# Five token streams in four groups at different phases, with a bf16 copy of the weights in DRAM

## The chip, the cores and the metric

The kernel runs on all 8 cores of one Trainium2 chip, the same program on each. Every core takes one prompt sequence (16 meta tokens and 2048 prompt tokens) and 16 of the 128 single-token samples, and computes the whole layer for them with all the weights. The time is that of the slowest core in device microseconds. Names: PE is TensorE's matmuls, PEld its weight loads, DVE is VectorE, ACT is ScalarE, POOL is GpSimd, SP is SyncE. A "slab" is one unit of weights, 128 partitions by up to 4096 columns, in a ring of slots in on-chip memory; POOL issues its transfer.

Some executions fall in a slower state: the four cores of a die, sometimes only two, show a lower mean clock (0.826 to 0.831 beside 0.974 to 0.976 on the other die in a run of 1937 us). "Fast" runs are those without it.

## The reference, cut to what matters

```python
def _layer(x, buf_a, buf_b, h0, p):
    x = x + 0.5 * _rmsnorm(_swiglu(_rmsnorm(x, p['g_ffn1_pre']), ...), p['g_ffn1_post'])      # FFN 1
    m, nba, nbb, hl = _mixer(_rmsnorm(x, p['g_mix_pre']), buf_a, buf_b, h0, p)                  # mixer
    x = x + _rmsnorm(m, p['g_mix_post'])
    x = x + 0.5 * _rmsnorm(_swiglu(_rmsnorm(x, p['g_ffn2_pre']), ...), p['g_ffn2_post'])      # FFN 2
    return x, nba, nbb, hl
# _mixer: u = h @ w_in, split into A_b | A_c | A_x | B_x | B_gate | gate_A | gate_B
#   y_a = (A_b * conv3(A_c * A_x)) @ w_out_a
#   y_b = (gelu(B_gate) * RG_LRU(conv4(B_x))) @ w_out_b          # a recurrence along the tokens
#   m   = (sigmoid(gate_A) * y_a + sigmoid(gate_B) * y_b) @ w_o
```

The model is 1024 wide and the FFNs 2816. The first half of the mixer is work for DVE and ACT (convolutions, gates, recurrence), the FFNs are almost all matmul. The recurrence forces the tokens of a sequence through that half in order.

## The kernel before

Three tiles of 688 to 704 tokens, each two streams of up to 352 columns. A tile goes through all its phases before the next one begins, and both streams are in the same phase. The program is a list of operations with their reads and writes, which a list scheduler in the program puts in an order for each engine at build time.

```python
TILES = [(0, 688, 0), (688, 688, 0), (1376, 688, 16)]
NSLOT = 5                                             # weight slots
...
def issue_unit(g, paced=True, dep=None):              # every slab: f32 in DRAM, cast to bf16 by the transfer
    dst = wring[:, slot, 0:n]
    src = wall[:, off:off + n]
    S.dma("pool", f"w{slot}", lambda e, dst=dst, src=src: e.dma_start(out=dst, in_=src),
          reads=(), writes=[("w", slot)], ..., extra_deps=extra)
...
def transpose_in(b, nr, dst_fn, dst_res_fn):          # inputs come token-major; PE turns them
    ...
    for kc in range(KC):
        ins = e.transpose(out, sview[0:nr, kc * 128:(kc + 1) * 128], ident[0:nr, 0:nr])
...
def evac_with_stats(bY, bS, sm, oc, dst32, dst_res, gain_col, first, last):
    act(sq, P[:, bY, 0:sm.n], AF.Square, ...)
    act(dst32[s][:, oc, 0:sm.n], P[:, bY, 0:sm.n], AF.Identity, ..., scale=gain_col)
    def stats():                                      # one ones-matmul for each of 8 blocks
        mm_group(bS, sm.n, [ones[:, :]], [sq], ..., start=first, stop=last)
...
for ti, (row0, nseq, nsamp) in enumerate(TILES):
    for sm in sms:
        norm_apply(sm, 0, rbuf_alt(sm))
    ffn(sms, 1, 2)
    mixer(ti, sms, nseq, T, 4)
    ...
    do_load(ti + 1)                                   # next tile's x, into the other of two buffers
    ffn(sms, 2, None)
    out_events += store_tile(row0, T, ns, extra_slots=last)
```

## Time and profile before

| | before |
|---|---|
| times of three runs, us | 1828.9, 1843.65, 1851.39 |
| span of the profiled slowest core, us | 1818.6 |
| PE busy / idle in it, us | 1663.4 / 155.2 |
| bf16 matmuls; f32 transposes | 10560; 304 |
| ACT table loads | 25 |
| slabs | 174, all f32 cast to bf16 |

The profile cuts the span into 40 equal slices. The two lines below are PE's busy tenths and the granted clock in tenths of full speed (9 is 90% or more):

```profile
PE   5999788898999899978889899989997978999997
...
PEclk7999899999999999989999999989998999999999
```

Each of the three tiles leaves the same mark: a few slices of 7 and 8 where both streams stand in the mixer's first half or change phase. That is what the change goes for. The DMA queues (packets, MB, share of the 16 engines' span) were half idle; q0 carries the slabs:

```profile
q0 software_dynamic: 25200, 167.26, 50.8%
q1 hardware_dynamic: 5244, 17.99, 2.9%
```

### The profile page before, as it was taken

How to read it: one execution, taken by the hardware profiler on the slowest of the kernel's cores; microseconds unless marked ns; L12 is line 12 of the kernel's file. 1: busy time of each engine (PE TensorE's matmuls, PEld its weight loads, DVE VectorE, ACT ScalarE, POOL GpSimd, SP SyncE). 2: the span in 40 equal slices, each digit the busy share in tenths (PEclk: the TensorE clock that was granted, in tenths of full speed). 3: DMA queues.
4: the chain of work that ended last, by engine and by line, in shares of the span. 5: the costliest groups of instructions: out<-in, count | busy, mean ns of one | idle time of the engine just before them, and what ended most of it. 6: DMA issues, size and time to landing. Idle time of an engine off the chain costs nothing.

```text
span 1818.6 us, 31211 instructions; the slowest of 8 cores (1806.5 to 1818.6 us)
## 1 busy us (share of the span) xinstructions
PE 1663.4 (91%) x10864; PEld 1083.4 (60%) x10864; DVE 761.8 (42%) x1660; ACT 788.1 (43%) x1631; POOL 93.0 (5%) x179
## 2 busy tenths in 40 slices
PE   5999788898999899978889899989997978999997
PEld 3666455565666666645556566666664545656665
DVE  3220789435220522078943522052207995343203
ACT  3212478657312312247865731231124777562122
POOL 0000000000000000000000000000000000000000
PEclk7999899999999999989999999989998999999999
DMA  7755633654655685543366365566555333745552
GB/s 157 128 102 105 116 71 70 115 112 93 117 102 96 135 160 95 105 92 70 70 117 114 90 116 102 96 135 135 93 100 99 68 73 69 141 80 107 98 96 78
DMA packets 30596, 187.23 MB, mean 103 GB/s; under 512 B 3430, under 2 KB 3686, under 8 KB 14316
## 3 DMA queue, kind: packets, MB, share of 16 engines
q0 software_dynamic: 25200, 167.26, 50.8%
q1 hardware_dynamic: 5244, 17.99, 2.9%
q8 instruction: 90, 1.47, 0.3%
q14 instruction: 62, 0.51, 0.1%
HBM read 343.54 MB, written 8.94 MB: 194 GB/s over the span
## 4 chain that ended last, share of the span: by engine, by line
PE 75%; DVE 9%; issue 8%; ACT 5%; DMA 2%; DVEq 0%; ACTq 0%; SPq 0%; POOLq 0%
PE P L455 73%; ACT B L475 3%; DVE hy L499 2%; DVE B L504 2%; DVE cbb L499 1%; DMA stg<-xin 1%; DMA wring<-wall 1%; PE P L584 1%; PE P L566 1%; ACT rstd L475 1%; DVE sgb L488 1%; DVE B L488 1%; DVE A L499 1%; ACT sqb L475 1%; DVE xsA L488 0%
## 5 line engine op out<-in xcount | busy, mean ns | idle before, releaser
L455 PE MATMUL P<-hy,wring 128*128 128x352 bf16 (+1 forms) x7296 | 1142.9, 317 | 79.7 <-DVE hy L499 24.5
L455 PEld LDWEIGHTS P<-hy,wring 128*128 128x128 bf16 x7296 | 721.6, 100 | 473.5 <-issue 99.6
L455 PE MATMUL P<-big,wring 128*128 128x352 bf16 (+1 forms) x2880 | 443.1, 310 | 0.0
L455 PEld LDWEIGHTS P<-big,wring 128*128 128x128 bf16 x2880 | 281.8, 98 | 141.4
L475 ACT ACTIVATE sgb<-P 128x352 f32<-128x352 f32 (+1 forms) x312 | 140.9, 458 | 479.0 <-PE P L455 465.5
L488 DVE TENSOR_TENSOR big<-P,sgb 128x352 bf16<-128x352 f32 (+1 forms) x264 | 136.7, 519 | 465.1 <-PE P L455 463.4
L475 ACT ACTIVATE B<-B 128x352 f32<-128x352 f32 (+3 forms) x318 | 183.4, 599 | 26.8 <-DVE B L499 10.1
L434 POOL DMA_DIRECT2D wring<-wall x174 | 92.3, 530 | 1678.6 <-PE P L455 1633.1
L475 ACT ACTIVATE sqb<-P 128x352 bf16<-128x352 f32 (+1 forms) x144 | 66.1, 459 | 242.9 <-PE P L455 242.8
L488 DVE TENSOR_TENSOR sgb<-hy,rstd 128x352 f32<-128x352 f32 (+1 forms) x96 | 45.4, 514 | 295.0 <-ACT rstd L475 295.0
L455 PE MATMUL P<-sqb,ones 128*128 128x352 bf16 (+1 forms) x288 | 86.9, 326 | 23.5 <-ACT sqb L475 21.5
L488 DVE TENSOR_TENSOR B<-P,B 128x352 f32<-128x352 f32 (+1 forms) x96 | 49.6, 519 | 136.5 <-PE P L455 123.0
L499 DVE SCALAR_TENSOR_TENSOR cbb<-bxb,par_sb,cbb 128x352 f32<-128x352 f32 (+2 forms) x152 | 82.6, 555 | 3.7 <-DVE SO L511 0.4
L475 ACT ACTIVATE B<-P 128x352 f32<-128x352 f32 (+2 forms) x106 | 47.8, 457 | 80.0 <-DVE hy L488 41.9
L455 PEld LDWEIGHTS P<-sqb,ones 128*128 128x128 bf16 x288 | 28.3, 99 | 53.0 <-issue 42.2
L499 DVE SCALAR_TENSOR_TENSOR A<-acx,par_sb,A 128x352 f32<-128x352 f32 (+2 forms) x104 | 56.9, 547 | 2.8
L475 ACT ACTIVATE sqb<-xsA 128x352 bf16<-128x352 f32 (+1 forms) x96 | 43.9, 488 | 29.9 <-PE P L455 15.0
L475 ACT ACTIVATE B<-P,dpar 128x352 f32<-128x352 f32 (+1 forms) x96 | 49.1, 546 | 10.9 <-PE P L455 9.7
L475 ACT ACTIVATE hy<-P,dpar 128x352 f32<-128x352 f32 (+1 forms) x96 | 52.2, 543 | 0.0
L488 DVE TENSOR_TENSOR xsA<-xsA,sgb 128x352 f32<-128x352 f32 (+1 forms) x96 | 45.6, 514 | 0.0
L475 ACT ACTIVATE B<-B,dpar 128x688 f32<-128x688 f32 (+1 forms) x48 | 41.7, 869 | 1.5
L504 DVE TENSOR_TENSOR_SCAN B<-B,CAR 128x688 f32<-128x688 f32 x24 | 39.6, 1648 | 0.8
(74 smaller groups left out, 700.9 us busy)
## 6 DMA issues: line engine op xcount, KB each, us to landing
wring<-wall POOLq DMA_DIRECT2D x126, 1024.0 KB, 8.7
wring<-wall POOLq DMA_DIRECT2D x48, 704.0 KB, 6.2
stg<-xin SPq DMA_DIRECT2D x13, 512.0 KB, 5.7
yout<-stg SPq DMA_DIRECT2D x12, 512.0 KB, 4.1
yout<-B SPq DMA_DIRECT2D x3, 512.0 KB, 2.7
B<-xin SPq DMA_DIRECT2D x2, 512.0 KB, 9.0
wrgs<-wrg POOLq DMA_DIRECT2D x1, 512.0 KB, 13.3
stout<-stg SPq DMA_DIRECT2D x1, 408.0 KB
```

The lines of the kernel that those rows point to most:

```text
L434: S.dma("pool", f"w{slot}", lambda e, dst=dst, src=src: e.dma_start(out=dst, in_=src), reads=(), writes=[("w", slot)], dur=2.0 + n * 128 * ...
L455: ins = e.matmul(out, lhs_list[k], rhs_list[k], start=(start and k == 0), stop=(stop and k == nk - 1))
L475: return S.op("act", lambda e: e.activation(out=out, in_=in_, func=func, **kw), reads=reads, writes=writes, dur=0.12 + 0.093 * nptr + fsz( ...
L488: return S.op(eng, lambda e: e.tensor_tensor(out=out, in0=in0, in1=in1, op=op), reads=reads, writes=writes, dur=vcost(eng, out, 2))
L499: return S.op(eng, lambda e: e.scalar_tensor_tensor(out=out, in0=in0, scalar=scalar, in1=in1, op0=op0, op1=op1), reads=reads, writes=write ...
L504: return S.op(eng, lambda e: e.tensor_tensor_scan(out=out, data0=d0, data1=d1, initial=init, op0=ALU.mult, op1=ALU.add), reads=reads, writ ...
L566: ins = e.transpose(out, sview[0:nr, kc * 128:(kc + 1) * 128], ident[0:nr, 0:nr])
L584: ins = e.transpose(out, srcs[kc], ident[:, :])
```

## The change

The intent is to let phases that need different engines lie side by side. The 2080 tokens become five streams of 414 to 418 columns in four groups (streams 0 and 1 are the first group), and the groups are a phase or two apart, so that one group's mixer runs beside another's FFN. Each group now reads all weights for itself, which would be 232 casts. So the first group casts and writes a bf16 copy back to DRAM, and the others read that copy, at half the bytes. Further: x comes and goes already transposed (the host reorders it), so the transposes go; the squares of the post-norms are added on DVE and summed by one ones-matmul instead of eight; scratch tiles come from pools that the scheduler assigns; three x buffers serve the five streams.

```diff
-TILES = [(0, 688, 0), (688, 688, 0), (1376, 688, 16)]
+SIZES = [418, 418, 416, 414, 414]
+GROUPS = [[0, 1], [2], [3], [4]]
+BUFSET = [0, 1, 2, 0, 1]
+NW = 5
+NF = 15
+SEGMENTS = [
+    [(0, "F1")],
+    [(0, "MAG"), (1, "F1")],
+    [(0, "MOW"), (1, "MAG")],
+    [(0, "F2"), (1, "MOW")],
+    [(1, "F2"), (2, "F1")],
+    [(2, "MAG"), (3, "F1")],
+    [(2, "MOW"), (3, "MAG")],
+    [(2, "F2"), (3, "MOW")],
+    [(3, "F2")],
+]
...
+def _nominal_order():                       # spreads the units of the pair over the stretch
+    ...
+            rate = (length - gap) / tot
+            for u, c in zip(us, cost):
+                out.append((t0 + gap + acc * rate, g, u, rate))
...
+        def issue_unit(g, u, prio):
+            src = wall if g == 0 else wsc
+            S.dma("pool", None, lambda e: e.dma_start(out=v[0:n](), in_=src[:, off:off + n]),
+                  [] if g == 0 else [("wsc", u)], [v], n * 128 * (4 if g == 0 else 2), prio=prio)
+            if g == 0:
+                S.dma("sp", iosem(), lambda e: e.dma_start(out=wsc[:, off:off + n], in_=v[0:n]()),
+                      [v], [("wsc", u)], n * 128 * 2, prio=prio)
...
-                    ins = e.transpose(out, sview[0:nr, kc * 128:(kc + 1) * 128], ident[0:nr, 0:nr])
+                S.dma("sp", iosem(), lambda e, dst=dst, src=src: e.dma_start(out=dst, in_=src), [],
+                      [R_xs(st, k) for k in range(k0, k0 + step)], step * st.n * 512)
...
-                mm_group(bS, sm.n, [ones[:, :]], [sq], reads=[("sqb", qb, s), "ones"], start=first, stop=last)
+            elif oc < KC - 1:
+                tt(sqs[0][0:m], sqs[0][0:m], sq[0:m], ALU.add, m, [sqs[0], sq], [sqs[0]])
+            else:
+                ...
+                mm_group(ps[0:m], m, [ones[:, :]], [sb_[0:m]], [sb_, "ones"], [ps])
```

MAG is the mixer's first half, MOW its second, F1 and F2 the FFNs; in the lists groups count from 0. Cuts are marked by "...".

## The prediction

> **What bounds the kernel now.** I read the spans of the cores first, then busy time by engine, the chain that ended last, PE's waits, the groups by shape, and at last the stretches with their granted clock. Cores and busy time:
>
> ```profile
> die 0 (median of its cores): 1809.3 us, clock 0.965
> die 1 (median of its cores): 1818.1 us, clock 0.959
> ```
>
> ```profile
> PE 1663.4 (91%) x10864; PEld 1083.4 (60%) x10864; DVE 761.8 (42%) x1660; ACT 788.1 (43%) x1631; POOL 93.0 (5%) x179
> ...
> PE 75%; DVE 9%; issue 8%; ACT 5%; DMA 2%; DVEq 0%; ACTq 0%; SPq 0%; POOLq 0%
> ```
>
> The dies agree within 1%, so the profile is a fast one. PE is busy for 91% of the span and makes 75% of the chain, so there are two things to win from: the 155 us in which PE stands (1818.6 - 1663.4), and PE time that is not matmul at full clock. The waits of PE say that no single producer is to blame; these three are the longest of some twenty kinds:
>
> ```profile
> PE P L455 <- DVE hy L499: 24.5, 9, 3.7
> PE P L455 <- ACT sqb L475: 21.5, 30, 2.1
> PE P L455 <- ACT sgb L475: 16.2, 5, 5.8
> ```
>
> They are the norms between phases and the mixer's chains: moments when both streams of a tile need ACT or DVE and PE has nothing else. The stretches (span, PE, PEld, DVE, ACT, POOL busy, clock, DMA share, GB/s) show where:
>
> ```profile
> 325.00:445.00 120.00, 115.06 (x764) 76.05 (x765) 51.41 (x105) 77.70 (x174) 5.28 (x10) 0.97 0.57 112
> 652.00:780.00 128.00, 128.00 (x881) 86.01 (x880) 19.24 (x42) 30.26 (x66) 8.44 (x16) 1.00 0.61 110
> 780.00:915.00 135.00, 106.36 (x650) 64.60 (x647) 115.50 (x248) 91.72 (x177) 5.38 (x10) 0.92 0.41 77
> 1380.00:1530.00 150.00, 119.20 (x706) 70.22 (x707) 129.48 (x338) 104.08 (x197) 5.28 (x10) 0.92 0.38 71
> ```
>
> The FFN (652 to 780) keeps PE full while DVE and ACT are at 15 and 24%. The first half of the mixer (780 to 915) has DVE at 86%, ACT at 68% and PE at 79%: 29 us of PE idle there, 31 us in the third tile's. Put side by side, the two would fill each other's gaps. The clock falls with the gaps; short stretches show its two low values:
>
> ```profile
> 788.00:792.00 4.00, 0.44 (x1) 0.10 (x1) 3.76 (x9) 0.98 (x2) 0.00 (x0) 0.50 0.01 2
> 632.00:636.00 4.00, 4.00 (x24) 2.42 (x23) 0.53 (x1) 1.39 (x3) 0.00 (x0) 0.81 0.96 181
> ```
>
> Read in 2 us steps over the whole span, this core has 96 us of steps at 0.50, all at or after a PE gap, and 48 us that include the 0.81 (two dense episodes of about 16 us, and a few mixed steps). PE busy time times (1 - clock) sums to 53 us.
>
> [...]128 us over 880 matmuls of 344 columns on average is 145.4 ns[...]. [...]The trace shows the 0.81, but does not show it held: 1.00 through 128 dense microseconds. [...]A weight slab reads 2 MB of f32 here and lands in 8.7 us[...], and I take rates from the trace.
>
> **The change part by part.**
>
> *Matmuls.* Per unit of weights there are five passes of 414 to 418 columns instead of six of 336 and 352. From the built programs I counted: before 10560 bf16 matmuls, 3.661 M columns, plus 304 f32 transposes; after 8695 matmuls, 3.604 M columns, no transposes (inputs and outputs come already transposed). After has fewer because the six streams become five, the squares of the post-norms are added on DVE and summed by one ones-matmul instead of eight, and the 16 meta columns are dropped after the recurrence; the halo of up to 4 columns in the mixer adds 2560. At full clock: before [...]1547 us; after [...]1520 us. **Gain 27 us.** The transposes' eleven groups add up to 48 us of PE busy time: **gain 48 us**. [...]
>
> *Clock.* The half-clock steps go with the gaps. With few gaps left I expect 25 to 30 us instead of 53. **Gain about 25 us.**
>
> *Check.* Before: 1547 + 48 + 53 = 1648 against 1663 busy, so 15 us (1%) of PE time is not explained; I allow 10 us for it after.
>
> *PE idle.* Before 155 us. Start: the chain has the first FFN matmul at 34.5 us, after loads of 5.75 and 10.91 us and transposes. After, four loads of 0.43 MB fill the first stream in perhaps 12 us beside the weights, then stats and rms (3 us) and eight 0.65 us multiplies: 20 us. End: after the last matmul 16 DVE passes of 0.59 us, rms and a store: 15 us (before 20). Between: the phases overlap, so the question is whether ACT and DVE can follow. Scaled from the rows at 336 and 352 columns to 418, an ACT pass from PSUM is 0.52 us (0.60 with a pointer scale or bias), from SBUF 0.55; a DVE tensor_tensor 0.59, scalar_tensor_tensor 0.65, the scan 1.09. One stream's first mixer half then costs ACT 64, DVE 63, PE 59 us; its second half ACT 35, PE 56; an FFN ACT 31 with norms, PE 92. Table loads: function families change 77 times in ACT's order after, against 25 loads before (1.28 us each), so 99 us. ACT in all: 5 x 159 + 99 = 893 us; DVE about 820. Both are near 55%, no bound as a whole. By pairing, in us:
>
> - mixer half 1 of group 0 (two streams) with FFN 1 of group 1: PE 212, ACT 176
> - mixer half 2 of group 0 with half 1 of group 1: PE 172, ACT 150
> - mixer half 1 of group 2 with FFN 1 of group 3: PE 151, ACT 110
> - mixer half 2 of group 2 with half 1 of group 3: PE 115, ACT 109, DVE 115 (the last stream has 96 short operations more)
>
> The last is a balance of three engines at 95 to 100% with chains between them: I expect 20 to 30 us of PE idle there, and 5 to 10 us in each of the others and at phase changes. Sum of idle: 20 + 15 + 25 + 25 = **85 us, gain 70 us.**
>
> *Weights.* Before: 174 casts, 50.8% of 1818.6 us over 174 = 5.3 us of all 16 engines each. After: 58 casts, 58 stores of the bf16 copy and 174 bf16 loads. Bytes at the wider side: 111 MB read + 56 written + 167 read = 334 MB, against 333 MB before; so the queues carry about the same, but the store and the reload cost half a cast each (2.7 us, an estimate by bytes). In the first phase group 0 asks 8.2 us of DMA (a full slab 5.5, its store 2.7) per 11.3 us of PE (64 x 0.176), in the later ones 5.4 us for a pair of units that take 11.3 us. Off the path in steady state. **Gain 0.** The slab ring stays at five for two groups, which is my worry here, but a bf16 slab should land in about 5 us.
>
> *Sum.* 1520 + 28 (clock) + 10 (unexplained) + 85 (idle) = 1643 if all is as feared, and 1520 + 20 + 0 + 65 = 1605 if the order, which was clearly tuned, holds. Middle: **1622 us of span**. The reported times exceed the profiled span: 1828.9 to 1851.4 against 1818.6, so 10 to 33 us. I add 15: **1637 us**, 11% less.
>
> **Rivals.**
> - [...]it appears twice on this core. Against: 325 to 445, with ACT at 65% and PE at 96%, ran at 0.97 with only its two ends below 1 (half clock after gaps). If 0.81 held for a fifth of the time: 0.2 x 1520 x 0.23 = 70 us, so about 1707.[...]
> - *ACT becomes the bound in the paired phases.* For: 77 table changes and 95% in one pairing. Against: 20% slack in three of four. If every pairing slips 15%, that is 0.15 x 650 = about 100 us, near 1700.
> - *The weight ring starves PE.* For: two groups share five slots, in one queue. Against: PE waited only 0.6 us for weights before, and demand is under 75% everywhere. A wait of 1 us for each of 232 slabs would cost 230 us; I give this little.
> - *All is hidden, PE is the only bound:* 1520 + 35 + 15, so 1570 of span, 1585 reported.
>
> **Range and chances.** 1590 to 1705: the low end is nearly no inner gap, the high end one of the first two rivals by its size. Slower needs a held 0.81 or a starved ring, 2%; within 2% (over 1807), 2%.
>
> **What would show it.** PE's matmul count 8695 and no transposes; PE busy near 1555; PE idle near 80, most of it at the two ends and in the last pairing; steps at 0.50 less than half of 96 us; DVE about 820 and ACT about 890 with some 77 table loads; PE waits on weights under 10 us. Wrong if the 0.81 fills more than a tenth of the span, or if the waits of PE name the weight ring or ACT's gates for over 100 us.

The sum: 1643 if all is as feared, 1605 if the order holds, 1622 of span and 1637 reported. What the trace of the kernel before shows is the rate from 652 to 780 us, 145.4 ns for 344 columns on average, or 0.423 ns a column; at that rate 3.661 M and 3.604 M columns come to 1547 and 1523, an estimate from this one stretch. The changed kernel ran near it: 477 matmuls of 414 columns, back to back from 969.68 to 1053.37 us, took 175.5 ns each, or 0.424 a column. That fewer matmuls save a fixed part of each was not shown. In the first rival, "it" is the granted clock of 0.81, seen from 632 to 646 and from 1224 to 1236 us. The 12 us for the first stream's loads and the 5 us for a bf16 slab are my estimates, for which I named no trace.

## The result, and the profile after

The changed kernel took 1695.2 us (median of four, 1694.31 to 1696.31), beside 1846.95 for the kernel before in the same rounds. The ratio is 0.930 (95% interval 0.926 to 0.935). Ratios here are the mean time of one kernel's fast runs over that of the other's fast runs of the same rounds, so not quite the ratio of the medians quoted. On a second chip the kernel before ran at 1813.7 and the changed one at 1697.0, ratio 0.935. So the gain is 6.5 to 7%, where 11% had been predicted. The first chip's runs of the kernel before, 1829 to 1851, lie 1 to 2% above the 1813 at which its undisturbed runs repeat on the chips used later, so 6.5% is the safer figure. The outputs are correct.

The dies agree, and the clock is higher than before:

```profile
die 0 (median of its cores): 1692.9 us, clock 0.976
die 1 (median of its cores): 1691.8 us, clock 0.977
```

Busy time by engine (share of the span, x instructions) and the chain of work that ended last (a name with q is that engine's sequencer):

```profile
PE 1560.4 (92%) x8695; PEld 847.6 (50%) x8695; DVE 775.8 (46%) x1444; ACT 841.6 (50%) x1519; POOL 123.3 (7%) x237
...
PE 79%; DVE 8%; DMA 6%; ACT 3%; issue 2%; SPq 0%; DVEq 0%; ACTq 0%; POOLq 0%
```

PE gave up 103 us of busy time (1663.4 to 1560.4), but only 22 us of idle time: 1693.3 - 1560.4 leaves 133 where before had 155. And in the chain the transfers went from 2 to 6%. The same two rows of slices as before:

```profile
PE   1999999999999998999995899999999997999795
...
PEclk9999999999999999999998799999999999999898
```

The mixer's marks are gone from the first 900 us. What is left sits in three places: the first slice, the middle (the 22nd and 23rd digit, at 890 to 970 us), and some spots in the last quarter. A table of stretches gives their size (start and end, length, then busy us of PE, PEld, DVE, ACT, POOL, each with its instructions, then clock, DMA share, GB/s):

```profile
0.00:50.00 50.00, 10.75 (x37) 3.95 (x38) 6.39 (x21) 11.15 (x21) 3.52 (x10) 1.00 0.96 194
50.00:900.00 850.00, 828.04 (x4661) 453.88 (x4662) 408.32 (x718) 462.96 (x845) 51.19 (x97) 0.99 0.69 178
900.00:950.00 50.00, 28.49 (x120) 12.89 (x118) 24.25 (x45) 19.48 (x32) 1.58 (x3) 0.73 0.71 202
950.00:1350.00 400.00, 393.33 (x2231) 215.85 (x2229) 193.34 (x377) 197.91 (x355) 40.11 (x76) 1.00 0.52 183
1350.00:1450.00 100.00, 86.59 (x463) 45.27 (x462) 69.09 (x156) 65.85 (x125) 6.87 (x14) 0.95 0.41 149
1450.00:1550.00 100.00, 100.00 (x572) 55.27 (x571) 22.56 (x39) 45.50 (x73) 10.56 (x20) 1.00 0.51 179
1550.00:1600.00 50.00, 38.26 (x198) 19.49 (x197) 29.50 (x53) 19.10 (x35) 3.69 (x7) 0.86 0.55 158
1600.00:1693.30 93.30, 74.96 (x426) 40.97 (x424) 22.36 (x39) 19.60 (x35) 5.82 (x11) 0.93 0.40 136
```

Length minus PE's time is PE's idle: 39.2 in the first 50 us, 22.0 in the next 850, 21.5 between 900 and 950, 6.7 in the next 400, 13.4 between 1350 and 1450, none in the next 100, 11.7 between 1550 and 1600, and 18.3 at the end. The sum is 132.9. PE's waits name what it stood for (us in total, times, longest):

```profile
PE P L535 <- ACT qp L549: 70.1, 24, 11.8
PE P L535 <- ACT fp L549: 16.6, 15, 4.1
PE P L535 <- DVE hy L567: 16.4, 4, 6.2
```

The first line must not be read as "ACT is slow". The tile `qp` holds the squares of the pre-norm, the first thing that is done with a freshly loaded x. At the start ACT makes these squares in pairs (start, duration, engine, operation, and in brackets the idle time before and what ended it):

```profile
7.33 0.99 ACT L549 ACTIVATE qp<-xs 128x418 bf16<-128x418 f32 x2 [1.96 <-DMA xs<-xin]
16.93 0.99 ACT L549 ACTIVATE qp<-xs 128x418 bf16<-128x418 f32 x2 [8.61 <-DMA xs<-xin]
23.87 0.99 ACT L549 ACTIVATE qp<-xs 128x418 bf16<-128x418 f32 x2 [5.95 <-DMA xs<-xin]
31.75 0.99 ACT L549 ACTIVATE qp<-xs 128x418 bf16<-128x418 f32 x2 [6.88 <-DMA xs<-xin]
```

ACT works 1 us and waits 6 to 9 for the next part of stream 0. The loads run beside slabs of 2 MB each, read for the ring, and the DMA share is 0.96. The first FFN matmul starts at 42.65:

```profile
42.65 5.29 PE L535 MATMUL P<-hy,wring 128*128 128x418 bf16 x24
```

The middle has the same form, for streams 3 and 4, whose x goes into the buffers that streams 0 and 1 are just leaving (first line: their results going out at SP's; second: the load behind it; then ACT's first squares):

```profile
902.92 0.39 SPq L631 DMA_DIRECT2D yout<-xs  x1
910.43 0.38 SPq L624 DMA_DIRECT2D xs<-xin  x1
...
921.00 1.86 ACT L549 ACTIVATE qp<-xs 128x414 bf16<-128x414 f32 x4 [8.50 <-DMA xs<-xin]
```

PE stood for 11.8 us before 921.7, and again 4.0, 4.2 and 1.5 us before 944.6. The queue shares grew as expected from the copy: the slabs' queue about as before, SP's larger by the stores.

```profile
q0 software_dynamic: 33552, 222.84, 48.4%
q1 hardware_dynamic: 17360, 73.43, 12.4%
```

### The profile page after: what moved, and what is told of

Read it like the earlier page. It is cut to its first block, busy times and chain, and to the rows that moved or that the text cites. A ratio compares the mean times of both kernels' runs of the same rounds, so it can differ in the third digit from the quotient of the medians.

```text
span 1693.3 us, 25995 instructions; the slowest of 8 cores (1687.0 to 1693.3 us)
## 1 busy us (share of the span) xinstructions
PE 1560.4 (92%) x8695; PEld 847.6 (50%) x8695; DVE 775.8 (46%) x1444; ACT 841.6 (50%) x1519; POOL 123.3 (7%) x237
## 3 DMA queue, kind: packets, MB, share of 16 engines
q0 software_dynamic: 33552, 222.84, 48.4%
## 4 chain that ended last, share of the span: by engine, by line
PE 79%; DVE 8%; DMA 6%; ACT 3%; issue 2%; SPq 0%; DVEq 0%; ACTq 0%; POOLq 0%
PE P L535 79%; DMA xs<-xin 3%; ACT fp L549 2%; DVE fp L553 2%; DMA yout<-xs 2%; DVE fp L567 2%; DVE xs L553 2%; DVE hy L567 1%; DMA wring<-wsc 1%; ACT L549 1%; DVE fp L572 1%; DMA xs<-stin 0%; DVE big L553 0%; ACT qp L549 0%; SPq L624 0%
## 5 line engine op out<-in xcount | busy, mean ns | idle before, releaser
L535 PE MATMUL P<-hy,wring 128*128 128x414 bf16 (+5 forms) x6080 | 1103.5, 341 | 39.4 <-DVE hy L567 16.4
L535 PEld LDWEIGHTS P<-hy,wring 128*128 128x128 bf16 x6080 | 592.7, 98 | 531.1 <-issue 64.5
L549 ACT ACTIVATE fp<-P 128x414 f32<-128x414 f32 (+4 forms) x530 | 267.3, 514 | 594.5 <-PE P L535 586.9
L535 PE MATMUL P<-big,wring 128*128 128x414 bf16 (+3 forms) x2400 | 435.8, 339 | 2.1 <-DVE big L553 1.1
L553 DVE TENSOR_TENSOR big<-P,fp 128x414 bf16<-128x414 f32 (+3 forms) x260 | 149.7, 588 | 381.5 <-PE P L535 339.1
L549 ACT ACTIVATE fp<-fp 128x414 f32<-128x414 f32 (+3 forms) x390 | 206.5, 545 | 33.1 <-DVE fp L567 12.1
L553 DVE TENSOR_TENSOR fp<-fp 128x414 f32<-128x414 f32 (+4 forms) x138 | 77.8, 565 | 211.1 <-ACT fp L549 209.5
L603 POOL DMA_DIRECT2D wring<-wsc x174 | 91.8, 528 | 1040.5 <-PE P L535 1040.5
L567 DVE SCALAR_TENSOR_TENSOR fp<-P,par_sb,fp 128x418 f32<-128x418 f32 (+3 forms) x120 | 77.4, 645 | 14.1 <-ACT fp L549 7.0
L553 DVE TENSOR_TENSOR xs<-xs,fp 128x414 f32<-128x414 f32 (+3 forms) x120 | 70.9, 591 | 12.8 <-DVE fp L553 0.5
## 6 DMA issues: line engine op xcount, KB each, us to landing
xs<-xin SPq DMA_DIRECT2D x4, 418.0 KB, 18.1
```

The costliest lines, as they stand in the source:

```text
L535: ins = e.matmul(o, ev(lhs_list[k]), ev(rhs_list[k]), start=(start and k == 0), stop=(stop and k == nk - 1))
L549: return S.op("act", lambda e: e.activation(out=ev(out), in_=ev(in_), func=func, **kw), reads, writes, dur, tbl=TBL.get(func), prio=prio)
L553: return S.op("dve", lambda e: e.tensor_tensor(out=ev(out), in0=ev(in0), in1=ev(in1), op=op), reads, writes, 0.153 + n / 960.0, prio=prio)
L567: return S.op("dve", lambda e: e.scalar_tensor_tensor(out=ev(out), in0=ev(in0), scalar=scalar, in1=ev(in1), op0=op0, op1=op1), reads, writ ...
L603: S.dma("pool", None, lambda e: e.dma_start(out=v[0:n](), in_=src[:, off:off + n]), [] if g == 0 else [("wsc", u)], [v], n * 128 * (4 if g ...
```

## The experiments

My theory after this: the missing gain is PE waiting for x, at the start behind weight slabs and in the middle behind the stores of the streams that used the buffer before, and the order of work at the phase changes of the last two groups. Rivals: that ACT's table loads stretch the norms, that the scheduler's idea of transfer times makes a bad order that a truer one would mend, that the bf16 copy or the removed transposes behave otherwise than assumed. Unless a chip is named, differences are between medians, against the 1697.0 us of the changed kernel run again, and a ratio is to the kernel before on the same chip. The runs came from four chips; the kernel before took about 1813 us on each when undisturbed, so times may be compared between them.

**The changed kernel again**, unedited, as the base on the second chip.

> The changed kernel again, unedited, as the yardstick for the other runs of this call. Both theories: within 0.5% of 1695 us, PE idle near 133 us, first FFN matmul near 42.6 us, a PE gap near 12 us just after 910 us.

1697.04 us, ratio 0.935 (0.933 to 0.937), correct. One of its four runs was slow: 1937 us, with the four cores of die 0 at a mean clock of 0.826 to 0.831.

### The start

**x first, first try.** Slabs 1 to 4 and the recurrence's gate weights wait for stream 0's x.

```diff
+            hold = [("xs", 0, k) for k in range(KC)] if g == 0 and 1 <= u < NW else []
             S.dma("pool", None, ...,
-                  [] if g == 0 else [("wsc", u)], [v], ...)
+                  hold if g == 0 else [("wsc", u)], [v], ...)
```

> Weight slabs 1 to 4 and the gate weights wait for the first stream's input to land; slab 0 does not. Theory (the input of the first stream lands late, at 32 us, because it shares the 16 DMA engines with five f32 slabs of 2 MB read each): first FFN matmul near 22 us instead of 42.6, time down by 15 to 20 us. Rival (the input load itself is slow, by its layout or its queue): input lands when it did, first FFN matmul no earlier than 38 us, time same or longer because the slabs come later.

1696.3 us: nothing. A miss of the experiment, not of the theory: POOL still issued five slabs within the first microseconds, because the scheduler, finding slabs 1 to 4 held, sent slabs 5 to 8 in their place. The x landed as late as before.

**x first, second try.** The same with `u >= 1`, so that every slab but the first waits.

> Repair of the earlier attempt, in which only slabs 1 to 4 were held and the scheduler simply sent slabs 5 to 8 ahead of them: now every slab but the first, and the gate weights, wait until the first stream's input has landed. Theory (input shares the DMA engines with the f32 slabs): first stream's input landed by 12 us instead of 31, first FFN matmul near 21 us instead of 41 to 43, time down by 12 to 20 us. Rival (the load is slow by itself): no earlier start, time equal or up.

1675.2 us (fast runs 1673.5 to 1675.8), ratio 0.923, correct: 22 us less. ACT's squares of stream 0 now come like this:

```profile
7.48 0.99 ACT L549 ACTIVATE qp<-xs 128x418 bf16<-128x418 f32 x2 [2.12 <-DMA xs<-xin]
16.10 2.04 ACT L549 ACTIVATE qp<-xs 128x418 bf16<-128x418 f32 x4 [7.62 <-DMA xs<-xin]
18.41 0.99 ACT L549 ACTIVATE qp<-xs 128x418 bf16<-128x418 f32 x2 [0.27 <-PE P L535]
```

All eight squares are done at 19.4 us, where they took until 32.7; the first FFN matmul starts at 26.5 instead of 42.7:

```profile
26.46 28.75 PE L535 MATMUL P<-hy,wring 128*128 128x418 bf16 x154
```

The slabs that were held back cost 4.8 us of PE waits in all. So the late first input is the cause of some 20 us.

### The middle

**A truer latency for the scheduler.** It counts 7 us more for the stores of x and for the loads of streams 3 and 4, so that it fills the gap with other matmuls.

```diff
+XLAT = 7.0
-                o.end = dma_free + DMA_LAT
+                o.end = dma_free + DMA_LAT + o.lat      # lat is XLAT for these loads and stores
```

> Only the order changes: the scheduler is told that input loads of streams 3 and 4 and all output stores take 7 us longer, which puts 32 of stream 2's matmuls ahead of stream 3's statistics; slab order stays. Theory A (PE idles after 910 us only because its fixed order puts statistics of a not yet loaded stream first): the 20 us of gaps between 910 and 945 go nearly entirely. Theory B (behind the order stands the weight ring: only three slabs of stream 2 are in its five slots, so PE has just 96 matmuls of 0.175 us to do meanwhile): only about 5 us go, since 32 matmuls are 5.6 us.

1695.1 us, no gain. 32 matmuls moved ahead of stream 3's squares, as intended, but now PE stood 13.7 us for the slab that these 32 need:

```profile
923.84 7.63 PE L538 MATMUL P<-hy,wring 128*128 128x416 bf16 x32 [13.66 <-DMA wring<-wsc]
```

**The same and group 2's first slabs 35 us later**, so that they don't lie in the gap.

```diff
+            if g == 2 and UNIT_LIST[us[0]][0] == "GU1":
+                gap = 35.0
```

> As the run before, and stream 3's first FFN is given a start 35 us later in the nominal order, so that more slabs of stream 2 are ahead of stream 3's in the ring: 160 matmuls of stream 2 (28 us) now stand before the first statistics of stream 3. Theory B: gaps between 910 and 945 fall from 20 us to under 5, time down 12 to 20 us against the changed kernel. If the load itself cannot be hidden (buffer freed too late for any order), the gap only moves to a later time and the total stays within 5 us.

1695.8 us, no gain. The gap splits into waits of 2 to 8 us, mostly for slabs. The stretch of it shows why:

```profile
905.00:945.00 40.00, 24.94 (x123) 12.46 (x120) 13.89 (x26) 10.81 (x19) 2.11 (x4) 0.81 0.97 259
```

The 16 DMA engines are busy for 97% of these 40 us. Neither of the two orders tried hides 3.4 MB of stores, 3.4 MB of loads and the slabs of two groups in this place; each only chose what waits.

**Streams 3 and 4 don't load** (a wrong result: they go on with what lies in the buffer).

```diff
         def load_x(st):
+            if st.i >= 3:
+                return
```

> Wrong result on purpose: streams 3 and 4 do not load their inputs but run on what streams 0 and 1 left in the two buffers; all stores stay. Takes away the wait (store, then load, into the same buffer) and 3.4 MB of traffic at the handover near 910 us. Theory (the handover is bound by moving x out and in): gaps between 905 and 960 fall from about 20 us to under 6, time down 14 to 22 us. Rival (slabs of the single-stream group are the limit there): gaps on the weight ring remain, time down less than 6 us.

1672.8 us, ratio 0.922: 24 us less. PE's lines at the place:

```profile
912.97 1.57 PE L535 MATMUL P<-hy,wring 128*128 128x416 bf16 x8 [0.76 <-ACT fp L549]
917.29 27.96 PE L535 MATMUL P<-hy,wring 128*128 128x414 bf16 x149 [2.76 <-DVE hy L567]
```

The longest wait there is 2.8 us, and then PE runs 149 matmuls without a break. So these loads are worth about 24 us. The run takes away the wait for the buffer and the traffic together, so it does not tell which of the two weighs more.

**A fourth x buffer**, on top of the held slabs, so that stream 3 can load early. Memory for it came from one weight slot (four) and four scratch tiles (eleven).

```diff
+XSET = [0, 1, 2, 3, 0]
-NW = 5
+NW = 4
-NF = 15
+NF = 11
```

> On top of holding the slabs behind the first input: a fourth x buffer, so that stream 3 loads long before the handover and stream 4 takes stream 0's buffer with 100 us to spare; paid for with four slab slots instead of five and 11 f32 scratch tiles instead of 15. Theory (store, then load of the same buffer makes the handover's idle time): gaps between 880 and 940 fall from 23 us to under 8, time 1675 minus 10 to 18. If the smaller ring or scratch costs as much: no gain.

Ratio 0.919 (0.911 to 0.927), correct. On this chip some cores were often at a lower clock; the runs that both dies ran undisturbed gave 1673 to 1677 us, against 1675 for the held slabs alone. On the profiled core, one of two at a lower clock (0.963 and 0.961), the wait for x turned into one for a slab:

```profile
PE P L537 <- DMA wring<-wsc: 12.9, 1, 12.9
```

But the cores differ. From 820 to 980 us PE idled 12 to 18 us on the six undisturbed cores, where it idled 20 to 24 on the cores of the run with the held slabs alone, and over the undisturbed runs the mean span of a core fell from 1670.5 to 1665.6 us. So the buffer helps the typical core; the slab waits differ from core to core (7.8 us on core 0, 13.8 on core 7), and the time is that of the slowest. Since the ring shrank at the same time, these runs do not show what a fourth buffer beside five slots would give.

### The other causes

**No table loads.** Silu and gelu issued as exp, a wrong result; ACT then never changes its function table.

```diff
+            hw = AF.Exp if func in (AF.Silu, AF.Gelu_apprx_tanh) else func
```

> Wrong result on purpose: silu and gelu are issued as exp, so that all of ACT's functions are of one family; every order stays as in the changed kernel. The 77 table loads (98.8 us of ACT) should go to 1 or 2. If ACT's table loads are off the path: time down by 0 to 8 us. If ACT bounds the paired phases: down by 25 us or more, and PE's waits on ACT outside the start fall by as much.

1689.0 us, ratio 0.931: 8 us less, for 76 loads and 100 us less of ACT:

```profile
PE 1562.8 (93%) x8695; PEld 848.4 (50%) x8695; DVE 776.3 (46%) x1444; ACT 741.8 (44%) x1443; POOL 123.3 (7%) x237
```

So some nine tenths of that ACT time did not cost time. ACT is not the bound.

**One group at a time.** Everything of the change stays but the pairing.

```diff
-SEGMENTS = [ ... ]
+SEGMENTS = [[(g, ph)] for g in range(4) for ph in ("F1", "MAG", "MOW", "F2")]
```

> The same five streams, slabs and copies, but a group runs all its phases before the next starts, so no phases are paired. Theory (the pairing is what keeps idle of PE low in spite of single streams): the mixer's first half and the norms of each single stream are exposed, about 60 us per single group and 30 for the pair, PE idle 133 + 150 to 250 us, time 1830 to 1950, that is no faster than before. Rival (pairing matters little, the gain is fewer matmuls and no transposes): under 1760 us.

1867.9 us, ratio 1.030, correct: slower than the kernel before by 3%, and 171 us slower than with the pairing. PE's busy line and longest wait:

```profile
PE 1602.1 (86%) x8695; PEld 849.4 (46%) x8695; DVE 775.4 (42%) x1444; ACT 795.3 (43%) x1475; POOL 123.5 (7%) x237
```

PE's idle time doubles to 264 us (1865.9 - 1602.1), and the half-clock steps go from 68 to 192 us. PE waited only 1.0 us for slabs in this run, so the ring is not the reason. The two phases at once carry the change; without them, the rest of it is slower than the kernel before.

**No bf16 copy.** All 232 slabs are cast from f32 again.

```diff
-            src = wall if g == 0 else wsc
+            src = wall
-            if g == 0:
-                S.dma("sp", iosem(), ... out=wsc ...)
```

> Every group casts its slabs from f32 in DRAM, no bf16 copy is stored or read: undoes one part of the change. By bytes at the wider side: 232 casts of 5.3 us (kernel before) is 1230 us of the 16 engines in 1695, against about 60% of the span now. If the copy only saves traffic that is hidden anyway: within 1% of 1696 us. If single-stream groups need it (a slab each 5.6 us of PE against 5.5 us of engines for a full cast): PE waits on the ring for 50 us or more, and the time rises by 5 to 15%.

The ratio of the runs counted as fast is 0.956 (0.945 to 0.968), correct. The one run with both dies undisturbed took 1734.1 us, against 1697 with the copy (1813 before on either chip): 37 us more. The queue of the slabs, and on an undisturbed core (5) its waits for them and the stretch from 950 to 1350 us:

```profile
q0 software_dynamic: 33552, 222.84, 75.5%
```

```profile
PE P L535 <- DMA wring<-wall: 23.1, 16, 4.5
950.00:1350.00 400.00, 375.49 (x2093) 203.56 (x2094) 174.09 (x324) 184.15 (x324) 37.48 (x71) 0.98 1.00 169
```

So a queue that is 75% busy over the span is not off the path: locally it was full, with the DMA engines busy for 100% of these 400 us (52% with the copy). The copy does not gain over the kernel before, it prevents this loss.

**Only the transposes, in the kernel before.** Its x comes and goes transposed by the host; nothing else changes. This is a part of the change done alone.

```diff
-                transpose_in(b, nr, ...)
+                xdma(lambda e, dst=dst, src=src: e.dma_start(out=dst, in_=src), [], ...)
```

> The kernel before with one part of the change alone: inputs and outputs come transposed from the host, so the 288 f32 transposes and their copies out of PSUM go; 16 of the states stay. The prediction's term says 46 us of PE busy time go; with part of the 34 us that PE waits for staged inputs and before transposes of outputs, the time should fall from 1813 by 50 to 75 us. Rival (the transposes sit in time that other waits would take anyway): less than 25 us.

Ratio 0.996 (0.987 to 1.004), with slow cores in most runs (mean clocks down to 0.835, beside 0.967): inconclusive as a time. On the undisturbed die its cores took about 1797 us against 1809 for the kernel before, 12 us less. PE's transposes are worth 48 us of busy time by their groups, but removing them brings new waits (the longest: 22.4 us for the first squares, 12.1 for a norm); the third line is ACT's first squares on an undisturbed core (5):

```profile
PE P L455 <- ACT sqb L475: 50.4, 41, 22.4
PE P L455 <- DVE hy L499: 48.8, 12, 12.1
22.20 0.88 ACT L475 ACTIVATE sqb<-xsA 128x352 bf16<-128x352 f32 x2 [17.09 <-DMA xsA<-xin]
```

So most of the 48 us had lain where PE would have stood anyway. The third line is the changed kernel's late first input again: ACT stands 17 us for x, and the first FFN matmul starts at 37.1 us, where in the kernel before, with its transposes, it started at 34.5.

**The second half of the mixer earlier.** For the last two groups, its units get the priorities of a stretch 25% shorter, so that the norms behind it lie beside the partner's matmuls instead of after them.

```diff
+            if g >= 2 and UNIT_LIST[us[0]][0] == "MO":
+                rate *= 0.75
```

> The changed kernel with one edit of its order: the second mixer half of groups 2 and 3 ends at three quarters of its paired phase. Theory (the norms after that half lie bare because both partners end together): the PE gaps of 6.2 us near 1426 and 1580, with the shorter ones before them, go; PE idle down from 133 to about 118, less time at half clock, time from 1696 to 1678 to 1686 us. Rival (the idle only moves into the last group's first mixer half): over 1690 us.

1670.4 us (1668.9 to 1671.6), ratio 0.919, correct: 27 us less, more than I had expected. The stretches where phases end:

```profile
1350.00:1450.00 100.00, 91.93 (x515) 49.09 (x514) 72.38 (x164) 74.06 (x134) 7.92 (x15) 1.00 0.47 165
...
1550.00:1600.00 50.00, 50.00 (x287) 27.58 (x286) 19.08 (x35) 15.43 (x25) 4.75 (x9) 1.00 0.84 230
```

PE's 86.6 and 38.3 us became 91.9 and 50.0 and the clock 1.00 in both. The two waits of 6.2 us for `hy`, eight multiplies of a norm with nothing beside them, are gone. Part of the gain is the clock: after such a wait PE's first 3 to 4 us ran at about 0.50 (in the changed kernel's trace 0.50 from 1426.4 to 1430 and from 1580 to 1583 us).

### Together

**The fourth buffer and the earlier second half**, and the same once more on another chip.

> As the run before, and the second mixer half of groups 2 and 3 is ordered to end at three quarters of its paired phase, so that the norms after it run while the partner still feeds PE. Should remove most of the two gaps of 6.2 us with their surroundings (about 8 and 12 us of PE idle near 1405 and 1560): 10 to 18 us less than the run before, near 1645 us. Rival: the paired mixer half 1 of the last group is bound by ACT and DVE (109 and 115 us for 115 of PE), and the idle time only moves there: less than 4 us.

> The combination again for a clean comparison, since one pair of cores of the last chip ran at a lower clock in most runs: first input ahead of the slabs, fourth x buffer, second mixer half early. Fast runs 1640 to 1650 us, ratio to the kernel before near 0.908. If the three parts do not add up on another chip: above 1660.

The first time one clean run of 1646.0 us, with the others disturbed (lowest mean clock of a core 0.970, 0.894 and 0.971; ratio 0.909, 0.897 to 0.920); on the other chip 1656.7 (fast runs from 1649.6), ratio 0.908 (0.905 to 0.912). Correct.

**The held slabs and the earlier second half, three x buffers.**

> The combination without the fourth x buffer, so with five slab slots and 15 scratch tiles again. If the fourth buffer is worth the smaller ring: 1658 to 1668 us, 10 to 20 more than the combination. If it only trades the wait for x for a wait for slabs: within 6 us of the combination.

1651.6 us (1650.8 to 1653.8), ratio 0.909 (0.906 to 0.912), correct. The fourth buffer gained nothing in the time of the slowest core that these runs can show (the mean core of the undisturbed runs took 1641.1 us with it and 1647.1 without), so this simpler version is the one to keep: 45 us below the changed kernel, by two edits of the order. PE idles 97.5 us of its 1649.6:

```profile
PE 1552.1 (94%) x8695; PEld 844.7 (51%) x8695; DVE 775.8 (47%) x1444; ACT 839.8 (51%) x1519; POOL 123.3 (7%) x237
```

What of the middle can be had stays open. Its loads cost 24 us in the run that leaves them out, neither order nor the fourth buffer took that back for the slowest core, and no run has a fourth buffer beside five slots.

## Why the prediction was right or wrong

The direction was right, and the time lies inside the range, near its upper end; the middle, 1637, was 58 us too low, and the gain of 11% was over half too large. As a ratio it is worse: 0.930 of the 1843.65 that the prediction started from is 1715, just above the range.

- **Matmuls: right.** 8695 matmuls, no transposes. PE's busy time came to 1560 us, where the sum if all was as feared had 1558 (1520 + 28 + 10). The parts moved: the clock cost 20 us (the steps at 0.50 went from 96 to 68 us), less than 28, and the unexplained rest was 20 instead of 10.
- **PE idle: the step that failed.** "Sum of idle: 20 + 15 + 25 + 25 = **85 us, gain 70 us**", with 65 in the hopeful case; it was 133. By its own terms:

| term | predicted | measured | by |
|---|---|---|---|
| start | 20 | 39 | idle in the first 50 us |
| end | 15 | 18 | idle after 1600, 15.5 of it after the last matmul |
| inner | 25 + 25 | 54 | 22.0 + 6.7 + 13.4 + 11.7 |
| x of streams 3 and 4 | not foreseen | 21.5 | idle from 900 to 950 |

The start failed at "four loads of 0.43 MB fill the first stream in perhaps 12 us beside the weights". They took about 30 us and 18.1 each at the median, because five slabs lay in the same engines; holding the slabs gave 22 us back, and PE then idled 19.2 us in the first 50, the 20 that were predicted. The middle was missing altogether: I counted transfers by their sum over the span and never asked what a buffer set used twice, three buffers for five streams, asks of one moment. Leaving the loads out gave 24 us. These two make 40 of the 48 us by which 133 exceeds 85.

- **Inner idle: the feared size was right** (54 for 50), its place was not. The last pairing, where three engines balance, had been given 20 to 30 us; from 1290 to 1410 us, roughly that pairing, PE idled 7. Much of the rest came at phase ends, from norms with nothing beside them: 8 us from 1410 to 1426 and 12 from 1550 to 1600. That the 27 us of the earlier second half could be had shows that the order was not as finished as "the order, which was clearly tuned" took it for.
- **Weights, gain 0: right as a comparison with before** (PE waited 4.8 us for slabs), but its reason was too easy. Demand "under 75% everywhere" is not harmless: at 75.5% of the queue, without the copy, the kernel lost 37 us. The bf16 slabs landed in 5.9 us at the median (1024 KB), where about 5 had been estimated. By the queue's share a cast took 5.7 us of the engines without the copy (75.5% of 1753.3 us over 232), and with it a bf16 load about 2.8 (48.4% of 1693.3 us, less 58 casts at 5.7, over 174), an estimate from the two traces, near the 2.7 of the prediction.
- **The 15 us added for the reported time: wrong.** The reported times exceeded the slowest core's span by about 2 us (1694.9 against 1693.3). The 10 to 33 us that I had read from the kernel before were scatter of its runs: on the second chip it ran at 1813.7. This error hid part of the other: 1622 of span was 71 us too low. With 2 us in place of 15 the range would have ended near 1692, below the measured 1695, so that the time lies inside it is luck.
- **The transposes' 48 us** went out of PE's busy time as predicted. That "gain" in the kernel before alone was about 12 us. In a sum of busy and idle both are consistent, but the idle term has to grow for what is uncovered.
- **Rivals.** The granted clock of 0.81 did not take over in the changed kernel's fast runs: the cores' mean clocks were 0.975 to 0.979, 400 us from 950 on ran at 1.00 in the profiled one, and in its trace the clock records of all eight cores hold only 1.00 and 0.50. (The few steps of 2 us near 0.81 lie singly beside half-clock steps and are a mean of the two.) In a disturbed run a clock near it does appear: in the profiled run of the combination's first time, cores 2 and 3 of die 0 ran at 0.83 from 360 to 510 us and cores 0 and 1 of the same die at 0.99. That the 0.826 to 0.831 on a whole die in the slow run of 1937 us is the same was not profiled and is not shown. ACT was no bound: 841.6 us with 77 table loads, some 50 below the 893 predicted (whose parts, 64 + 35 + 2 x 31 per stream, give 161 and not 159), and without the loads only 8 us. DVE had 775.8, where about 820 were predicted. The ring starved PE for 4.8 us.

The stretch of the disturbed run on core 2 and on core 0, with the same busy time for PE but 701 against 820 matmuls:

```profile
360.00:510.00 150.00, 145.59 (x701) 74.86 (x699) 82.54 (x145) 91.78 (x172) 9.19 (x17) 0.83 0.55 146
360.00:510.00 150.00, 145.59 (x820) 79.97 (x819) 95.64 (x169) 105.28 (x200) 10.60 (x20) 0.99 0.67 174
```

Start 22, middle 24, order 27 and tables 8 us, each taken alone, sum to 81, of the size of the 71 us missing from the span. The sum is no proof, since such gains may overlap; the first and third, 48.4 us alone, gave 45.5 together.

## What to carry to other kernels

Two phases side by side pay (171 us here), but only where the data is there: for each moment at which a new input must come, at the start and wherever a buffer is used again, add up all bytes in flight and the rate measured under that load, not the share over the span. Hold back transfers that are not needed yet when the first input decides, and check that the scheduler does not send others in their place. And put the end of a phase, where norms run alone, well before the end of its partner's.
